# Splitting the normalised input once per layer instead of once per sweep

## The chip, the cores and the metric

The kernel runs on one core of a Trainium2 chip. The metric is the device time of one execution in microseconds (us). A core has five engines, each with its own queue of instructions, which it takes in order: TensorE (PE; PEld is its weight load), VectorE (DVE), ScalarE (ACT), GpSimd (POOL) and SyncE (SP). In this kernel all transfers between DRAM and the memory on the chip are issued by SP.

## What is computed

The reference is a trunk of two layers over 2048 tokens of width 1024. Each layer normalises its input, projects it once, and hands the columns to four groups of heads:

```python
h = rms_norm(x, ln_g)
proj = jnp.einsum('bsd,dn->bsn', h, w_in)
(a_q, a_k, a_v, a_g, b_cq, b_ckv, b_kr, b_g,
 c_q, c_k, c_v, c_g, c_iq, c_ik, c_iw, d_q, d_k, d_v, d_g) = jnp.split(proj, split_points, axis=-1)
y_a = stick_breaking(...)          # group A
y_b = softmax_attention(...)       # group B, queries and keys from normed latents
y_c = dsa_attention(...)           # group C, softmax over the 256 keys that an indexer scores highest
y_d = rms_norm(diff_attention(...), diff_subln_g) * (1.0 - lam_init)   # group D
y = jnp.concatenate([silu(a_g) * y_a, silu(b_g) * y_b, silu(c_g) * y_c, silu(d_g) * y_d], axis=-1)
return x + jnp.einsum('bsn,nd->bsd', y, w_out)
```

All of it is float32.

## The kernel before

**Products in two parts.** TensorE multiplies numbers in a rounded form of float32 (`F32R`). To keep float32 accuracy the kernel splits both factors: `hi` is the number rounded, `lo` is what the rounding leaves, and a projection (`proj`, lines 256, 257 and 260) sums hi·hi, hi·lo and lo·hi: for each of eight blocks of 128 features two matmuls with the block of `h_hi`, then eight more with `h_lo`. `split` (line 195) makes the parts: a copy that rounds, by GpSimd (`pcopy`, line 193) or ScalarE (line 200), and a subtraction, by GpSimd (`psub`, line 187) or VectorE (line 204).

**Sweeps.** The tokens are 16 tiles of 128. A layer is seven sweeps over the tiles, in the order `a h d0 d1 b c o`. Sweep a normalises and transposes the input (`a_load`), does group A and the indexer's scores, and starts the searches for the 256 highest scores. Sweep h makes the latents of group B and the gates of A and B. Sweeps d0 and d1 do two heads of group D each, and the gates of C and D. Sweep b is group B's attention, c is group C's, and o is the output projection. The last searches run in sweeps h and d0 (`SEARCH`), on ScalarE (line 538, a count of scores by their sign) and VectorE (lines 601 to 622, steps on a few numbers per token).

**Where the input goes.** `a_load` leaves the normalised, transposed tile `hf` in the buffer `x4a` (lines 331 to 334), stores it to a DRAM tile `hT` (line 335), and splits it for its own use (line 337): on GpSimd, but for the very first tile. The sweeps h, d0, d1 and c, four in each layer and so 128 times in all, load `hT` into `x4a` again (line 234) and split it again (line 236). Who splits is set by hand: ScalarE and VectorE (`"ad"`) take the even tiles in h, tiles 0 to 6 in d0, 4 to 10 in d1 and 4 to 9 in c, which is 28 tiles of a layer's 64; GpSimd (`"pp"`) takes the other 36.

**Buffers.** `x4a` is one buffer of 4 KB per partition and serves other uses too (the input tile of `a_load`, the mask of group C, the tile of sweep o). `h_hi` and `h_lo` are two buffers each, so that a third tile's parts can be written only when the first's projection has read its own. A tile's load is asked for four tiles ahead of its attention, the projection three, and the transposes to the attention's layout two (`drive`).

**Order.** `drive` interleaves the generators of loads, projections, transposes and attention by costs written into them, and a scheduler that simulates the program (`schedule_with_timeline_sim=True`) then sets the order on each engine. In a d sweep a tile's projection (`proj_d`) is followed by the root mean square of its heads (`rs`, lines 271 and 272, on GpSimd), the rotation tables (`tab`, line 190, GpSimd), the rotation on VectorE, and the split of queries and keys into `hl` (lines 997 and 998, GpSimd by lines 193 and 187). TensorE's transposes of `hl` (line 283) wait for that. GpSimd also does a fifth of the difference of the two softmaxes (lines 1070 and 1071, `rw`).

Of the kernel before, what the change touches and what calls it, by code (L numbers as in the profile page):

```python
# [10 lines left out]
F32 = mybir.dt.float32  # L11
# [49 lines left out]
def merge(*gens):  # L61
    """Interleaves generators, whose first item is their whole cost and whose others are costs of steps."""
    act = []
    for g in gens:
        if g is None:
            continue
        tot = next(g)
        act.append([0.0, max(tot, 1.0), g])
    while act:
        a = min(act, key=lambda t: t[0] / t[1])  # L70
        try:
            a[0] += next(a[2])
        except StopIteration:
            act.remove(a)
# [15 lines left out]
class Share:  # L90
    """A generator taken in shares of its cost."""
# [16 lines left out]
class Trunk:  # L108
    def __init__(self, ctx, tc, I, out, layers=2):
# [11 lines left out]
        self.hT = [dt([128, KT, 128], F32, name=f"hT{i}") for i in range(NT)]  # L121
# [40 lines left out]
    def g2(self, shape, dtype=F32):  # L162
        """scratch of the projections, up to 2 KB"""
        return self.wk.tile(shape, dtype, name="g2", bufs=4)

    def pt(self, shape, dtype=F32):
        """scratch of the attention's inner loops, up to 2 KB"""
        return self.wk.tile(shape, dtype, name="pt", bufs=3)

    def o2(self, shape, dtype=F32):  # L170
        """scratch of the attention's results, up to 2 KB"""
# [23 lines left out]
    def split(self, hi, lo, raw, eng="pp"):  # L195
        """hi: raw rounded, lo: what that leaves"""
# [9 lines left out]
    def weights(self, W, key, src, pieces, n, kt=KT, first=False):  # L206
        """src [kt*128, cols] in DRAM; pieces (column, count) side by side make n columns."""
# [3 lines left out]
        for k in range(kt):  # L211
            # the very first ones come all at once, through the memory of the rows
# [15 lines left out]
    def early(self, i, n):  # L228
        """who splits: ScalarE and VectorE while the attention of tile i leaves them time, else GpSimd"""
        return "ad" if FROM <= i < n else "pp"  # L230

    def get_h(self, i, eng="pp"):
        hf = self.x4("a", [128, KT, 128])
        self.nc.sync.dma_start(hf, self.hT[i])
        hi, lo = self.h_tiles()
        self.split(hi, lo, hf, eng)
        return hi, lo

    def load_h(self, l, i, st):
        yield 1.0  # L240
        st["h", i] = self.get_h(i, "pp" if i % 2 else "ad")

    def load_c(self, l, i, st):
        yield 1.0
        st["h", i] = self.get_h(i, self.early(i, EARLY[0]))

    def load_d(self, l, i, st):
        yield 1.0
        st["h", i] = self.get_h(i, self.early(i + 4 * (FROM > 0 and st["half"] == 0), EARLY[1]))
# [13 lines left out]
    def rstd(self, who, ss, n, width):  # L263
        """(ss / width + eps) ** -0.5 of [128, n]"""
# [10 lines left out]
    def transposes(self, dst, srcs, eng="act", tag="pj"):  # L275
        """srcs: up to four [128, m] fp32 views; dst [m, len, 128] view."""
# [3 lines left out]
        # sources of rounded results are rounded themselves  # L280
# [8 lines left out]
    def piece(self, st, key, i, shape, dtype=F32):  # L289
        """the tile of key that holds token tile i, of four each; last but one dim of shape is 4 tiles long"""  # L290
# [5 lines left out]
    def at(self, offset, g):  # L296
        """generator g, its instructions scheduled as if they came offset instructions later"""
# [17 lines left out]
    def a_load(self, l, i, st):  # L315
        """x tile -> normalised, transposed, split"""
# [18 lines left out]
        nc.sync.dma_start(self.hT[i], hf)  # L335
        hi, lo = self.h_tiles()
        self.split(hi, lo, hf, "ad" if l == i == 0 else "pp")
        st["h", i] = hi, lo
# [19 lines left out]
    def functions_a(self):  # L358
        """has ScalarE take the set of functions with both exponential and logarithm"""
        self.nc.scalar.preload_act_table_set("natural_log_exp_and_others")  # L360

    def a_first(self, l, i, st):
# [33 lines left out]
        for r in range(2):  # L396
# [6 lines left out]
            if zr is not None:  # L403
                # what is left of the stick after these blocks is at most exp(X0 - z0)
# [63 lines left out]
    def hilo64(self, u):  # L468
        """u [128, 5, 64]: [hi lo] of the first four, [hi hi] and [lo lo] of the last"""
# [9 lines left out]
    def ci_score(self, l, i, st, tied=True):  # L479
        """scores of tile i into a row buffer"""  # L480
# [3 lines left out]
        # the general search takes two more rows  # L484
# [3 lines left out]
        for c0 in range(0, n, 512):  # L488
            w = min(512, n - c0)
            # equal scores of zero rank by their index  # L490
# [25 lines left out]
    def ci_search(self, l, b):  # L516
        """per row of the tiles of b a threshold with 249..256 scores at or above it, then the 256th itself"""
# [17 lines left out]
        def count(dst, th):  # L535
            """number of scores at or above th"""
# [922 lines left out]
```

## Time and profile before

| | us |
|---|---|
| median of three runs | 4274.78 |
| lowest and highest | 4272.74, 4277.41 |
| the profiled execution, its span | 4276.6 |

The profiled execution has its span as its time: the instructions run from its first to its last microsecond. Its sweeps are told apart by the instructions that only one of them has. In the first layer, a runs to about 447 us, h to 660, d0 to 960, d1 to 1257, b to 1627, c to 1946 and o to 2145; in the second layer, a ends at 2560, h at 2787, the two d sweeps at 3085 and 3377, b at 3746, c at 4063. The projections of a sweep's first tiles lie in the sweep before.

How to read the rows: a row of a timeline is an instruction with its start and length; what stands in brackets is how long its engine stood still before it and what ended that. The chain of waits follows the program back from its last instruction, at each step to what released it. PEclk is the clock that TensorE was granted, as a share of 2.4 GHz; the other level is 1.2 GHz, so that 0.62 is a stretch that was mostly at the lower one.

### The profile page before, as it was taken

The numbers are of one execution on the slowest core, as the hardware profiler recorded it, in microseconds if no ns is written. First come the engines' busy times: TensorE is split into PE (matmuls) and PEld (weight loads), VectorE is DVE, ScalarE is ACT, GpSimd is POOL, SyncE is SP. The second block draws the span as 40 slices with busy tenths as digits, with TensorE's granted clock in tenths as the row PEclk, the third lists the DMA queues.
The fourth block names the chain that finished last, engine by engine and source line by source line (L and its number), as shares of the span: only waits on it lengthen the run. The fifth ranks groups of instructions, "written<-read, shape, count | busy, mean of one in ns | idle before, by whom it ended". The sixth has DMA issues, their size and how long they took to land.

```text
span 4276.6 us, 75274 instructions
## 1 busy us (share of the span) xinstructions
PE 3937.6 (92%) x25833; PEld 3249.9 (76%) x25833; DVE 2906.3 (68%) x10326; ACT 2371.9 (55%) x4846; POOL 1650.7 (39%) x2350
## 2 busy tenths in 40 slices
PE   6999996899988999999989999979999889999999
PEld 6877786777866777777878787867788667777777
DVE  3798788787875655663337988887968766555622
ACT  3656677465665545454126667765666655554621
POOL 2333423665664433420033343337747544344100
PEclk9999997899988999999999999979999899999999
DMA  3222531121110002114522225311211100021144
GB/s 104 80 77 84 175 112 58 50 59 52 50 35 26 19 23 68 50 44 139 167 88 81 81 91 172 114 54 48 61 53 49 36 22 18 26 74 46 59 138 139
DMA packets 204842, 312.60 MB, mean 73 GB/s; under 512 B 63777, under 2 KB 147873, under 8 KB 203937
## 3 DMA queue, kind: packets, MB, share of 16 engines
q1 hardware_dynamic: 204448, 307.69, 22.7%
q8 instruction: 206, 3.38, 0.3%
q14 instruction: 188, 1.53, 0.1%
HBM read 211.89 MB, written 95.72 MB: 72 GB/s over the span
## 4 chain that ended last, share of the span: by engine, by line
PE 57%; DVE 20%; ACT 6%; POOL 6%; DMA 5%; issue 5%; SPq 0%; DVEq 0%; ACTq 0%; POOLq 0%
PE y L866 9%; PE s L837 8%; PE tp L283 7%; PE pj L256 7%; PE pj L257 6%; PE pj L260 6%; PE s L256 3%; PE s L257 3%; PE s L260 3%; ACT junk L538 2%; DVE sc L506 2%; DVE rw L843 2%; PE pj L283 2%; DMA w_raw<-w_in 2%; DVE rw L841 2%
## 5 line engine op out<-in xcount | busy, mean ns | idle before, releaser
L256 PE MATMUL pj<-w_hi,h_hi 128*128 128x384 f32 (+4 forms) x2560 | 880.2, 352 | 51.5 <-POOL w_hi L193 22.9
L257 PE MATMUL pj<-w_lo,h_hi 128*128 128x384 f32 (+4 forms) x2560 | 863.9, 345 | 8.0 <-DVE w_lo L204 4.0
L847 ACT ACTIVATE rw<-rw,at_mn 128x896 f32<-128x896 f32 (+15 forms) x512 | 615.7, 1204 | 173.1 <-DVE at_mn L846 148.2
L285 ACT COPY pt<-tp 128x512 f32<-128x512 f32 (+3 forms) x689 | 358.1, 529 | 467.8 <-PE tp L283 390.3
L256 PEld LDWEIGHTS pj<-w_hi,h_hi 128*128 128x128 f32 x2560 | 505.7, 198 | 88.9 <-POOL w_hi L193 26.0
L283 PE MATMUL tp<-ident,rw 128*128 128x128 f32 x3264 | 540.4, 287 | 34.4 <-DVE rw L1074 20.3
L257 PEld LDWEIGHTS pj<-w_lo,h_hi 128*128 128x128 f32 x2560 | 505.3, 197 | 32.4 <-DVE w_lo L204 6.6
L260 PE MATMUL pj<-w_hi,h_lo 128*128 128x384 f32 (+4 forms) x2560 | 523.4, 338 | 0.0
L283 PEld LDWEIGHTS tp<-ident,rw 128*128 128x128 f32 x3264 | 365.4, 143 | 172.2 <-issue 117.5
L843 DVE TENSOR_SCALAR_CACHE_REDUCE rw<-s 128x512 f32<-128x512 f32 x576 | 383.0, 684 | 108.2 <-PE s L837 73.7
L260 PEld LDWEIGHTS pj<-w_hi,h_lo 128*128 128x128 f32 x2560 | 434.1, 190 | 25.7 <-issue 10.8
L271 POOL TENSOR_SCALAR rs<-ss 128x2 f32<-128x2 f32 (+4 forms) x224 | 61.7, 276 | 802.8 <-DVE ss L987 202.7
L538 ACT ACTIVATE junk<-sg,st_T 128x1152 int8<-128x1152 f32 (+4 forms) x224 | 293.9, 1312 | 83.9 <-DVE st_T L622 56.9
L272 POOL TENSOR_TENSOR rs<-rs,mhalf 128x8 f32<-128x8 f32 (+5 forms) x256 | 317.0, 1239 | 16.9
L287 DVE COPY pt<-tp 128x512 f32<-128x512 f32 (+3 forms) x247 | 152.9, 619 | 197.6 <-PE tp L283 163.5
L837 PE MATMUL s<-dk,qa 96*128 96x512 f32 (+3 forms) x640 | 233.5, 424 | 43.9 <-DVE rw L843 22.3
L187 POOL TENSOR_TENSOR h_lo<-x4a,h_hi 128x1024 fp32r<-128x1024 f32 x103 | 255.5, 2480 | 39.4 <-PE pj L260 22.8
L193 POOL TENSOR_SCALAR hl<-g 128x256 fp32r<-128x256 f32 (+1 forms) x384 | 151.2, 408 | 286.9 <-DVE g L452 61.3
L837 PE MATMUL s<-bk,qa 128*128 128x512 f32 (+6 forms) x960 | 257.8, 394 | 1.2 <-DVE at_mn L841 0.7
L283 PE MATMUL pj<-identr,hl 128*128 128x128 f32 (+1 forms) x1280 | 174.6, 258 | 74.1 <-POOL hl L187 47.9
L193 POOL TENSOR_SCALAR h_hi<-x4a 128x1024 fp32r<-128x1024 f32 x103 | 115.2, 1119 | 319.8 <-PE pj L257 156.1
L841 DVE CUSTOM_DVE_ANT_0 rw<-s,maskR 128x128 f32<-128x128 f32 (+3 forms) x400 | 187.7, 478 | 56.7 <-PE s L837 55.5
(267 smaller groups left out, 8731.5 us busy)
## 6 DMA issues: line engine op xcount, KB each, us to landing
x4a<-hT SPq DMA_DIRECT2D x128, 512.0 KB, 3.5
x4a<-x SPq DMA_DIRECT2D x32, 512.0 KB, 3.5
hT<-x4a SPq DMA_DIRECT2D x32, 512.0 KB, 2.6
x4a<-y SPq DMA_DIRECT2D x32, 512.0 KB, 3.5
x4b<-gate SPq DMA_DIRECT2D x32, 512.0 KB, 3.6
x4c<-x SPq DMA_DIRECT2D x32, 512.0 KB, 4.1
y<-o SPq DMA_DIRECT2D x96, 128.0 KB, 2.1
w_raw<-w_in SPq DMA_DIRECT2D x48, 192.0 KB, 2.6
```

The lines of the kernel that those rows point to most:

```text
L256: nc.tensor.matmul(p[:, :n], hi[:, k, :], whi[k], start=(k == 0), stop=False)
L257: nc.tensor.matmul(p[:, :n], hi[:, k, :], wlo[k], start=False, stop=False)
L260: nc.tensor.matmul(p[:, :n], lo[:, k, :], whi[k], start=False, stop=(k == kt - 1))
L272: nc.gpsimd.tensor_tensor(r, r, self.mhalf[:, :n], op=OP.pow)
L283: nc.tensor.transpose(p[:m, j, :].bitcast(dst.dtype), s.bitcast(dst.dtype), ident)
L285: nc.scalar.copy(dst, p[:m, :len(srcs), :])
L538: nc.scalar.activation(self.junk[:, :ns[g]], Sg[g], AF.Sign, bias=th[:, g:g + 1], scale=-1.0, accum_out=dst[:, g:g + 1])
L837: nc.tensor.matmul(p[:, :w], x, y, start=(k == 0), stop=(k == len(ops) - 1))
L841: nc.vector.tensor_tensor_reduce(o, p[:, :w], b, -scale, 3.0e38, OP.add, OP.min, m)
L843: nc.vector.tensor_scalar(o, p[:, :w], -scale, None, op0=OP.mult, op1=OP.min, accum_out=m)
L847: nc.scalar.activation(rw, rw, AF.Exp, bias=mn, scale=-1.0, accum_out=ls)
L866: nc.tensor.matmul(y[o:o + 64, :], v(j), pt[:, c * m:(c + 1) * m, :].rearrange("p a b -> p (a b)"), start=(j < 2), stop=(j >= nb - 2), ski ...
```

## The change

The DRAM tile `hT` becomes twice as large and holds both parts. `a_load` splits first, and then stores `h_hi` and `h_lo`, in two transfers of 512 KB where there was one. The four later sweeps load both parts straight into `h_hi` and `h_lo`, in two transfers of 512 KB where there was one, and split nothing. The choice of who splits falls away.

```diff
-        self.hT = [dt([128, KT, 128], F32, name=f"hT{i}") for i in range(NT)]
+        self.hT = [dt([128, 2, KT, 128], F32, name=f"hT{i}") for i in range(NT)]
...
-    def get_h(self, i, eng="pp"):
-        hf = self.x4("a", [128, KT, 128])
-        self.nc.sync.dma_start(hf, self.hT[i])
+    def get_h(self, i):
         hi, lo = self.h_tiles()
-        self.split(hi, lo, hf, eng)
+        for j, t in enumerate((hi, lo)):
+            self.nc.sync.dma_start(t.bitcast(F32), self.hT[i][:, j])
         return hi, lo

     def load_h(self, l, i, st):
         yield 1.0
-        st["h", i] = self.get_h(i, "pp" if i % 2 else "ad")
+        st["h", i] = self.get_h(i)
...
     def load_c(self, l, i, st):
         yield 1.0
-        st["h", i] = self.get_h(i, self.early(i, EARLY[0]))
+        st["h", i] = self.get_h(i)

     def load_d(self, l, i, st):
         yield 1.0
-        st["h", i] = self.get_h(i, self.early(i + 4 * (FROM > 0 and st["half"] == 0), EARLY[1]))
+        st["h", i] = self.get_h(i)
...
         for c in range(2):
             nc.vector.tensor_mul(hf[:, 4 * c:4 * c + 4, :], ps[c],
                                  self.gain[l][:, 4 * c:4 * c + 4, None].to_broadcast([128, 4, 128]))
-        nc.sync.dma_start(self.hT[i], hf)
         hi, lo = self.h_tiles()
         self.split(hi, lo, hf, "ad" if l == i == 0 else "pp")
+        for j, t in enumerate((hi, lo)):
+            nc.sync.dma_start(self.hT[i][:, j], t.bitcast(F32))
         st["h", i] = hi, lo
```

The rest of the diff takes out comments, so that lines after 225 stand one lower or one higher than before. The order of instructions changes in three places that matter here.

On GpSimd, in sweep d0 of the first layer, these rows stood in one run before (`rs` root mean squares, `tab` rotation tables, `hl` split queries and keys of one tile; `h_hi` and `h_lo` the split input of a later tile):

```order
L272 TENSOR_TENSOR rs<-rs,mhalf 128x8
L272 TENSOR_TENSOR rs<-rs,mhalf 128x2
L193 TENSOR_SCALAR h_hi<-x4a 128x1024
L190 TENSOR_TENSOR tab<-ci_cs,gain 128x2x32 x2
L187 TENSOR_TENSOR h_lo<-x4a,h_hi 128x1024
L193 TENSOR_SCALAR hl<-g_8751 128x4x64
L193 TENSOR_SCALAR hl<-g_8751 128x4x2x32
L187 TENSOR_TENSOR hl<-g_8751,hl 128x4x32 x2
```

and the same tile's rows stand so now:

```order
L271 TENSOR_TENSOR rs<-rs,mhalf 128x8
L271 TENSOR_TENSOR rs<-rs,mhalf 128x2
L190 TENSOR_TENSOR tab<-ci_cs,gain 128x2x32 x2
L193 TENSOR_SCALAR hl<-g_8721 128x4x64
L193 TENSOR_SCALAR hl<-g_8721 128x4x2x32
L187 TENSOR_TENSOR hl<-g_8721,hl 128x4x32 x2
```

The two rows of the input's split are gone, and nothing has taken their place between `tab` and `hl`.

On SP, in sweep a of the first layer, one tile's transfers stood so before (`sc` scores, `y` results of group A, `x4a<-x` the next input tile, `sg` scores for a search, `ci_cs` rotation tables; in brackets what SP waits for, the DMA lanes among it):

```order
L512 DMA sc_172<-sc 128x768 [waits DMAHW5_49,DVE_49]
L433 DMA y_92<-o_2152 128x256 [waits Activation_49]
L320 DMA x4a<-x 128x1024 [waits DMAHW4_49,PE_49,Pool_49]
L524 DMA sg<-sc_172 128x768 [waits DMAHW5_49,DMAHW0_49]
L446 DMA ci_cs<-c_rope 128x128 [waits DMAHW1_49,DVE_49]
L335 DMA hT_79<-x4a 128x1024 [waits DMAHW2_49,DVE_49]
```

and stand so now:

```order
L512 DMA sc_172<-sc 128x768 [waits DMAHW4_49,DVE_49]
L433 DMA y_92<-o_2160 128x256 [waits Activation_49]
L337 DMA hT_78<-h_lo 128x1024 [waits DMAHW6_49,Pool_49]
L319 DMA x4a<-x 128x1024 [waits DMAHW7_49,PE_49]
L524 DMA sg<-sc_172 128x768 [waits DMAHW4_49,DMAHW0_49]
L446 DMA ci_cs<-c_rope 128x128 [waits DMAHW1_49,DVE_49]
L337 DMA hT_79<-h_hi 128x1024 [waits DMAHW2_49,Pool_49]
L337 DMA hT_79<-h_lo 128x1024 [waits DMAHW3_49,Pool_49]
```

The store waits for GpSimd's split where it waited for VectorE's product, and the store of `h_lo` stands ahead of the next tile's load.

On SP in sweep d0 a load stood so before (`gate` the gates of a tile, `out_of` a search's result):

```order
L234 DMA x4a<-hT_77 128x1024
L1099 DMA y_87<-o_8446 128x128
L1168 DMA gate_123<-g_8645 128x256
L234 DMA x4a<-hT_78 128x1024
L1027 DMA ci_cs<-c_rope 128x2x32
```

and stands so now:

```order
L1168 DMA gate_123<-g_8617 128x256 [waits DMAHW5_49,Activation_49]
L1027 DMA ci_cs<-c_rope 128x2x32 [waits DMAHW6_49,Pool_49]
L1099 DMA y_88<-o_8595 128x128 [waits DMAHW7_49,DVE_49]
L642 DMA out_of_195<-ge 128x1664 [waits DMAHW0_49,DVE_49]
L235 DMA h_hi<-hT_78 128x1024 [waits DMAHW1_49,PE_49]
L235 DMA h_lo<-hT_78 128x1024 [waits DMAHW2_49,PE_49]
L1168 DMA gate_124<-g_8792 128x256 [waits DMAHW3_49,Activation_49]
```

Both loads wait for TensorE, which has to have read the pair of buffers that they fill, and stand ahead of the store of the gates that the same tile's projection ends with.

## Rows read from the trace of the kernel before

**Rows 1.** Page, parts 1 and 4: engines' busy time; last-ending chain by engine.

```profile
PE 3937.6 (92%) x25833; PEld 3249.9 (76%) x25833; DVE 2906.3 (68%) x10326; ACT 2371.9 (55%) x4846; POOL 1650.7 (39%) x2350
PE 57%; DVE 20%; ACT 6%; POOL 6%; DMA 5%; issue 5%; SPq 0%; DVEq 0%; ACTq 0%; POOLq 0%
```

**Rows 2.** Windows h, d0, d1, first layer: us, busy (count) per engine, PEclk, DMA.

```profile
447.00:660.00 213.00, 195.29 (x913) 164.49 (x912) 170.43 (x803) 154.60 (x303) 67.96 (x87) 0.97 0.43 141
660.00:960.00 300.00, 256.93 (x1732) 223.82 (x1732) 246.93 (x923) 183.46 (x382) 167.24 (x230) 0.86 0.18 54
960.00:1257.00 297.00, 275.80 (x2046) 231.03 (x2046) 236.24 (x798) 190.74 (x418) 176.98 (x246) 0.96 0.15 46
```

**Rows 3.** Tiles h_hi, h_lo: engine, operation, count, ns min/median/max of the splits.

```profile
L193 POOL TENSOR_SCALAR h_hi<-x4a x103: 1040/1048/1477, 51.0 to 3935.9; 128x1024 fp32r<-128x1024 f32 x103
L200 ACT CAST h_hi<-x4a x57: 1028/1047/1066, 29.9 to 3829.5; 128x1024 fp32r<-128x1024 f32 x57
L187 POOL TENSOR_TENSOR h_lo<-x4a,h_hi x103: 2347/2410/4387, 52.1 to 3939.9; 128x1024 fp32r<-128x1024 f32 x103
L204 DVE TENSOR_TENSOR h_lo<-x4a,h_hi x57: 1196/1224/1496, 31.6 to 3830.9; 128x1024 fp32r<-128x1024 f32 x57
```

**Rows 4.** Chain by line: 660 to 1257, 2787 to 3377, 1627 to 1946 us.

```profile
by line: PE pj L256 10.4%; PE pj L257 9.6%; PE pj L260 8.5%; PE y L866 7.7%; issue 6.9%; PE tp L283 6.1%; DVE rw L843 5.8%; PE s L837 5.7%; DVE rw L1074 3.1%; ACT junk L538 2.9%; POOL rs L272 2.7%; DVE rw L841 2.6%; POOL h_lo L187 2.5%; PE 
by line: PE pj L256 10.0%; PE pj L257 9.1%; PE pj L260 7.9%; PE y L866 7.2%; issue 6.4%; DVE rw L843 6.3%; PE tp L283 6.0%; PE s L837 5.1%; DVE rw L1074 3.1%; DVE rw L841 2.8%; POOL h_lo L187 2.5%; ACT rw L847 2.5%; POOL rs L272 2.2%; POOL 
by line: PE y L866 18.8%; PE tp L283 18.1%; PE s L837 14.6%; PE pj L256 5.9%; PE pj L257 5.6%; PE pj L260 5.4%; DVE rw L841 4.2%; issue 3.5%; DMA w_raw<-w_out 2.2%; PE y L878 1.9%; PE pj L283 1.8%; DVE h_lo L204 1.7%; DMA x4a<-out_of 1.4%; 
```

**Rows 5.** Timeline in d0, GpSimd, then TensorE: start us, us, what [idle before].

```profile
744.59 1.04 POOL L193 TENSOR_SCALAR h_hi<-x4a 128x1024 fp32r<-128x1024 f32 x1
...
746.32 2.38 POOL L187 TENSOR_TENSOR h_lo<-x4a,h_hi 128x1024 fp32r<-128x1024 f32 x1
748.66 2.54 POOL L193 TENSOR_SCALAR hl<-g 128x256 fp32r<-128x256 f32 x2
751.17 0.87 POOL L187 TENSOR_TENSOR hl<-g,hl 128x128 fp32r<-128x128 f32 x2
...
751.68 0.66 PE L283 MATMUL pj<-identr,hl 128*96 128x128 f32 x4 [2.90 <-POOL hl L187]
```

**Rows 6.** Window around Rows 5, columns as in Rows 2.

```profile
742.00:753.00 11.00, 4.99 (x31) 3.76 (x30) 10.96 (x18) 2.25 (x5) 10.04 (x10) 0.62 0.28 92
```

**Rows 7.** Line 602 over the whole run; two instructions of sweep h, timeline.

```profile
L602 DVE TENSOR_SCALAR st_dn<-st_T x112: 149/161/2422, 151.3 to 2846.8; 128x2 f32<-128x2 f32 x112
...
524.30 2.43 POOL L187 TENSOR_TENSOR h_lo<-x4a,h_hi 128x1024 fp32r<-128x1024 f32 x1
524.33 2.42 DVE L602 TENSOR_SCALAR st_dn<-st_T 128x2 f32<-128x2 f32 x1
```

**Rows 8.** Pieces of the chain in order of time: start us, us, what.

```profile
467.94 2.31 DVE st_L L577
...
568.97 2.43 DVE st_T L622
```

**Rows 9.** TensorE's waits, 660 to 1257 us: total us, times, longest.

```profile
PE pj L283 <- POOL hl L187: 18.8, 14, 5.4
```

**Rows 10.** Timeline of TensorE in sweep h: one pair's last use, its next first use.

```profile
555.34 2.03 PE L260 MATMUL pj<-w_hi,h_lo 128*128 128x512 f32 x8
...
568.88 0.44 PE L256 MATMUL pj<-w_hi,h_hi 128*128 128x416 f32 x1
```

**Rows 11.** DMA queue: packets, MB, share; transfers of tile hT to landing.

```profile
q1 hardware_dynamic: 204448, 307.69, 22.7%
...
DMA to landing us min/median/max: 2.6/3.4/8.5
```

**Rows 12.** SyncE's waits over the whole run: total us, times, longest.

```profile
SPq L335 <- DVE x4a L333: 144.9, 21, 13.9
SPq L320 <- DMA hT<-x4a: 36.8, 15, 3.7
```

## The prediction

> **What bounds the kernel now.** I read the page first, then the windows by sweep, then the chain of waits in the sweeps that the change touches, then the timeline at its largest pieces. On the page TensorE's matmuls are busy 92% of the span, VectorE 68%, and the chain that ended last lies 57% on PE, 20% on DVE, 6% each on ACT and POOL and 5% on DMA [rows 1]. That is an average. By sweeps, b and o hardly touch what is changed, and the d sweeps are where PE is held up: of d0's 300 us its matmuls are busy 257, of d1's 297 they are busy 276, so 64 us of standstill in the first layer's two, and the granted clock is 0.86 and 0.96 there [rows 2]. In sweep h, PE stands still for 18 us of 213 [rows 2].
>
> What holds PE up in the d sweeps is seen in one place. From 744.6 us GpSimd runs the rounding copy of a later tile's input, 1.04 us, and its subtraction, 2.38 us, ahead of the split of the present tile's queries and keys, for which PE's transposes wait; PE stands still 2.90 us before them [rows 5]. In the 11 us around it GpSimd is busy 10.0, VectorE 10.96, PE 5.0, and the granted clock is 0.62, so mostly 1.2 GHz [rows 6]. So the input's split does lie on the path there, though no page total shows it.
>
> **The change, part by part.**
>
> *What goes.* 128 splits. GpSimd did 103 in all, of which 31 are group A's own and stay: 72 x (1.048 + 2.410) = 249 us off GpSimd. ScalarE did 57 copies and VectorE 57 subtractions, of which one each stays: 56 x 1.047 = 59 us and 56 x 1.224 = 69 us [rows 3]. Most of it ran beside PE's work, so these 377 us are no forecast; what counts is the part on the chain.
>
> *Piece 1, GpSimd in the d sweeps.* GpSimd's subtraction of the split is 2.5% of the chain in the first layer's d sweeps (597 us) and 2.5% in the second's (590 us) [rows 4]: 14.9 + 14.8 = 29.7 us.
>
> *Piece 2, VectorE stopped by GpSimd.* In sweep h, a search step on two numbers per token, 0.161 us at the median, took 2.42 us: it began 0.03 us after GpSimd's subtraction of 2.43 us and ended with it [rows 7]. The chain of the first layer's sweep h holds four such pieces of 2.31 to 2.43 us, the first and the last of which are shown [rows 8]: 4 x (2.35 - 0.16) = 8.8 us. The second layer's h runs on PE by its chain, so I count none there.
>
> The Trainium skill (SBUF — State Buffer, "Who interferes with whom") states that a VectorE instruction in a two-port mode, or one with two SBUF inputs, and a GpSimd instruction block each other for the whole of whichever came first, and that transfers block no engine. The trace agrees on the first: 2.42 us beside 2.43 [rows 7]; on the second no run here says anything. By that rule every VectorE instruction of these kinds that meets a split gets shorter, not the four alone, which speaks for the first rival below.
>
> *Piece 3, sweep c.* VectorE's subtraction of the split is 1.7% of the chain over the first layer's 319 us of sweep c [rows 4]: 5.4 us, and I take the same for the second layer: 11 us.
>
> *What of this comes back.* 29.7 + 8.8 + 11 = 49.5 us on the chain. When a piece goes, what was second latest sets the time. The one place that shows how much is gained is the standstill above: PE stood 2.90 us where the split had taken 3.42 us of GpSimd [rows 5], which is 0.85. It is one of the larger standstills, so I round down to 0.8: 40 us. From below, TensorE's transposes in the first layer's d sweeps waited for `hl` 18.8 us in 14 waits [rows 9], and only some of those have a split ahead of them; if a quarter does, both layers give 9 us.
>
> *What is added: transfers.* 128 loads and 32 stores of 512 KB more, 84 MB beside the 307.7 MB that take 22.7% of the 16 engines' span [rows 11]; at the same price, 6 points more. Each load of 512 KB lands in 3.4 us at the median, 8.5 at most [rows 11]. I take 7 us for the two parts together, and 8.5 as the bad case. What hides this is the second pair of buffers. In sweep h, where a tile is shortest, the last use of one pair ends at 555.34 + 2.03 = 557.4 us and the same pair is needed at 568.9 [rows 10]: 11.5 us, in which the load fits. (The rounded part is free earlier, and the rest is needed later than that.) In the d sweeps tiles are longer: 16 in 300 us, 19 us each [rows 2]. Cost: nothing. Were that cover gone, the loads would cost up to 3.5 us a tile, 128 times. Below nothing I see no effect of the loads.
>
> *What is added: waits.* SP now stands at each load until PE has read the pair. Behind it stand the store of the gates, which the same projection ends with, rotation tables for the next tile and results. They become due at about that moment or are wanted a tile later; I take nothing, and up to 0.3 us a tile, 40 us, for the far end, from the waits that SP has at such places now (36.8 us in 15 waits at one, some 2.5 us each [rows 12]). The store in sweep a now waits for GpSimd's split; that is a rival below. The next tile's load into `x4a` no longer waits for the store to land, 36.8 us of SP's time [rows 12], which lies off the path as far as rows show; I take nothing.
>
> *What moves.* The order on PE changes in sweeps a, d0, d1 and c, and not in b and o. The same d sweeps take 597 us in one layer and 590 in the other, with the same work in another order [rows 4]; so I give the order 10 us either way, and no sign.
>
> **Sum.** 4276.6 - 40 = 4236.6 for the profiled execution. Its span is 1.8 us above the median of the runs, so I forecast 4235 us by the median, 0.9% less; between 4215 and 4266 I call it this case.
>
> **The rivals.**
>
> *The relief is larger, by the clock.* The windows of d0 and d1 have 0.86 and 0.96 of the clock [rows 2]: 300 x 0.14 + 297 x 0.04 = 54 us a layer that PE has lost, 108 in both. If all 49.5 us come back, with GpSimd's copy beside its subtraction (1.05 of 2.41 x 29.7 = 13 us), and a quarter of the clock's loss, 27 us: 4275 - 90 = 4185 us. For it: in the window around the standstill VectorE and GpSimd are both full [rows 6], and the clock is low in that very place. Against it: most of the 64 us has other causes, the softmax's rows on DVE first (line 843 is 5.8% of that chain [rows 4]).
>
> *It is hidden.* What PE waited for arrives no earlier, since VectorE's rotation, not GpSimd, sets when `hl` can start. Then the lower bound holds, 9 us or less: 4266 to 4275. For it: PE's waits for `hl` are 18.8 of 64 us [rows 9]. Against it: in the case shown GpSimd had no pause from the copy to `hl` [rows 5].
>
> *Slower: the stores of sweep a hold SP.* SP stands at the old store 144.9 us, waiting for VectorE's product [rows 12]. The new stores wait 1.05 and 2.41 us longer, for the split [rows 3], and behind the second stands the next tile's input load. 32 tiles x 3.46 = 111 us if all of it lies on the path. Against it: that load waited for the same split before, since it fills the buffer that the split reads. It decides from the point at which SP comes to a tile's tables or input later than that tile's first matmuls want them; with half the tiles, 55 us lost and 40 gained: 4290 us.
>
> **How the numbers follow.** The forecast 0.45, larger relief 0.25, hidden 0.16, slower by the stores or by a worse order in the same sweeps 0.14. The range reaches from the first rival's 4185 to the edge of the slower case: 4184 to 4282; below lies 0.07, above 0.13. A measurement here tells about 0.2%, 8.5 us: faster means under 4266, slower over 4283. The first two cases are faster, and a little of the hidden one: 0.71; the hidden case's rest 0.15; slower 0.14.
>
> **What would show it.** Right: 72 fewer splits on GpSimd; TensorE's waits for `hl` in the first layer's d sweeps under 12 us; no search step in sweep h at 2.4 us, unless beside a weight's split; d windows of 597 and 590 us some 12 to 18 us shorter each, h 4 to 8 us shorter in the first layer, c some 4 each, b and o within 2; granted clock of d0 above 0.86; TensorE waiting under 10 us in all for loaded parts. Wrong: sweep a longer by over 10 us in a layer, with SP at the stores and PE or ACT waiting for the input load or tables; PE waiting for a load in h; or d windows unchanged with the waits for `hl` gone and VectorE's rows in their place.

## The result

The kernel after takes 4235.6 us by the median of four runs (4221.5 to 4242.2); the kernel before took 4275.4 beside it. The ratio is 0.9897, 95% interval 0.9877 to 0.9917: faster by 1.0%. The forecast was 4235.

The rows of the page of after that answer to [rows 1, 3, 11]: the span, the busy time of each engine with its share and instructions, the DMA queue (packets, MB, share of 16 engines), and issues with KB each and us to landing.

```profile
span 4230.8 us, 75339 instructions
...
PE 3925.9 (93%) x25833; PEld 3246.6 (77%) x25833; DVE 2789.1 (66%) x10270; ACT 2318.9 (55%) x4790; POOL 1363.8 (32%) x2206
...
q1 hardware_dynamic: 227488, 391.59, 29.3%
...
h_hi<-hT SPq DMA_DIRECT2D x128, 512.0 KB, 3.8
h_lo<-hT SPq DMA_DIRECT2D x128, 512.0 KB, 4.9
```

PE is busy 12 us less, at the same count. GpSimd has 144 instructions and 287 us less, ScalarE 56 and 53, VectorE 56 and 117. The queue moves 84 MB more and is busy 6.6 points more.

The windows of after, columns as in [rows 2] (us, busy time and instructions of PE, PEld, DVE, ACT, POOL, the granted clock, DMA share, GB/s): the first layer's h, both its d sweeps together, the second layer's, the first layer's c, and last the first 300 us of the first layer's d sweeps, to set beside d0.

```profile
435.00:651.00 216.00, 200.00 (x939) 170.12 (x937) 148.51 (x754) 143.09 (x295) 45.00 (x75) 0.96 0.57 178
651.00:1238.00 587.00, 529.64 (x3775) 455.15 (x3775) 461.68 (x1769) 370.03 (x795) 265.85 (x436) 0.92 0.27 80
2758.00:3338.00 580.00, 528.14 (x3803) 453.77 (x3803) 458.50 (x1668) 353.25 (x779) 270.14 (x452) 0.92 0.27 82
...
1606.00:1922.00 316.00, 305.08 (x2191) 231.75 (x2191) 186.60 (x605) 170.69 (x316) 83.13 (x132) 0.99 0.26 81
...
651.00:951.00 300.00, 260.99 (x1780) 227.56 (x1780) 243.03 (x1008) 192.89 (x396) 125.49 (x212) 0.89 0.29 86
```

The d sweeps take 587 and 580 us where they took 597 and 590 (from the sweep's first matmul, as in the table below, 587 and 579 where they took 595 and 590). The clock changed little: 0.89 in the first 300 us, where d0 had 0.86 [rows 2], and 0.92 over both sweeps, where it was 0.91; in the second layer's it was 0.93 and is 0.92. By these windows the first layer's h is not shorter: 216 us, where it took 213 [rows 2]. What is shorter is the sweep a ahead of it, 435 us where it took 447.

TensorE's waits for `hl`, total us, times, longest. First the kernel before in the second layer's d sweeps, 2787 to 3377 us (the first layer's 18.8 is [rows 9]):

```profile
PE pj L283 <- POOL hl L187: 20.5, 14, 5.6
```

then after in the first layer's d sweeps, 651 to 1238 us, and in the second's, 2758 to 3338 us:

```profile
PE pj L282 <- POOL hl L187: 7.6, 5, 3.1
...
PE pj L282 <- POOL hl L187: 13.7, 9, 3.2
```

39.3 us have become 21.3. What is left has no split of the input in it. GpSimd's timeline in d0 of after ahead of the longest of these waits in the first layer (start us, us, instruction, in brackets idle time before it and what ended that), and TensorE's transposes that wait:

```profile
743.55 0.20 POOL L270 TENSOR_SCALAR rs<-ss 128x8 f32<-128x8 f32 x1 [9.00 <-DVE ss L987]
743.84 1.64 POOL L271 TENSOR_TENSOR rs<-rs,mhalf 128x8 f32<-128x8 f32 x1
745.44 0.78 POOL L190 TENSOR_TENSOR tab<-ci_cs,gain 128x64 f32<-128x64 f32 x2
...
747.01 0.78 POOL L193 TENSOR_SCALAR hl<-g 128x256 fp32r<-128x256 f32 x2
747.75 0.70 POOL L271 TENSOR_TENSOR rs<-rs,mhalf 128x2 f32<-128x2 f32 x1
748.42 0.87 POOL L187 TENSOR_TENSOR hl<-g,hl 128x128 fp32r<-128x128 f32 x2
...
748.93 1.09 PE L282 MATMUL pj<-identr,hl 128*96 128x128 f32 x8 [3.07 <-POOL hl L187]
```

GpSimd was idle for 9 us and waited for VectorE's sum of squares (`ss`). In [rows 5] it had no pause: the input's split stood in front. But [rows 5] is not how most of the waits before came about. By GpSimd's timeline, its split stood ahead of `hl`, without a pause of GpSimd over 0.3 us in between, in 10 of the 28 waits of both layers' d sweeps, 12.9 of the 39.3 us. The longest of [rows 9], 5.4 us, came so (VectorE, GpSimd, TensorE of the kernel before):

```profile
723.79 1.22 DVE L204 TENSOR_TENSOR h_lo<-x4a,h_hi 128x1024 fp32r<-128x1024 f32 x1
...
725.54 0.42 DVE L1043 TENSOR_TENSOR g<-g,x4c 128x256 f32<-128x256 f32 x1
...
728.02 0.41 DVE L991 TENSOR_TENSOR g<-g,rs 128x256 f32<-128x256 f32 x1
...
728.60 0.78 POOL L193 TENSOR_SCALAR hl<-g 128x256 fp32r<-128x256 f32 x2 [3.13 <-DVE chkC L641]
...
729.85 0.66 PE L283 MATMUL pj<-identr,hl 128*96 128x128 f32 x4 [5.42 <-POOL hl L187]
```

GpSimd stood idle for 3.13 us, and what it waited for was the rotation (lines 1043 and 991) on VectorE, with VectorE's own subtraction of a later tile's input, and search and softmax work, in between.

The search steps. Line 602 over the whole run of after (the answer to [rows 7]), and two instructions of its sweep a that still meet:

```profile
L602 DVE TENSOR_SCALAR st_dn<-st_T x112: 149/161/296, 150.9 to 2798.2; 128x2 f32<-128x2 f32 x112
...
157.86 2.41 POOL L187 TENSOR_TENSOR h_lo<-x4a,h_hi 128x1024 fp32r<-128x1024 f32 x1
157.89 2.41 DVE L603 TENSOR_SCALAR st_nd<-st_T 128x2 f32<-128x2 f32 x1
```

Which step meets a split is the order's doing, so the count says more than one line. Of the steps on two numbers per token, 24 took over 1.5 us before, 16 in the sweeps a and 8 in h; after, 11 do, all in sweep a, where GpSimd's own split for that sweep remains. In the runs below, 21 to 24 do in each kernel with all splits and 9 to 13 in each with none; with GpSimd's alone taken away 11, with the others' alone 21.

Last, SyncE's waits over the whole run of after (total us, times, longest), to [rows 12]:

```profile
SPq L235 <- PE pj L256: 611.0, 96, 18.0
SPq L337 <- POOL h_hi L193: 245.9, 31, 17.3
```

These are the largest rows of each line; all rows together, SP stands at the loads (line 235) for 834 us and at the stores (line 337) for 296. Among TensorE's waits of the whole run, no row names a loaded part, so that standing doesn't reach it through the loads. Something behind SP does come later: VectorE's waits for a search's results (`out_of`, line 630) grow from 7.8 to 23.4 us. No run shows whether that costs time.

### The profile page after: what moved, and what is told of

Same layout as the page of the kernel before. It is cut to its first block, busy times and chain, and to the rows that moved or that the text cites. A ratio compares the mean times of both kernels' runs of the same rounds, so it can differ in the third digit from the quotient of the medians.

```text
span 4230.8 us, 75339 instructions
## 1 busy us (share of the span) xinstructions
PE 3925.9 (93%) x25833; PEld 3246.6 (77%) x25833; DVE 2789.1 (66%) x10270; ACT 2318.9 (55%) x4790; POOL 1363.8 (32%) x2206
## 5 line engine op out<-in xcount | busy, mean ns | idle before, releaser
L259 PE MATMUL pj<-w_hi,h_lo 128*128 128x384 f32 (+4 forms) x2560 | 535.9, 339 | 0.0
L270 POOL TENSOR_SCALAR rs<-ss 128x2 f32<-128x2 f32 (+4 forms) x224 | 49.9, 223 | 1074.7 <-DVE ss L911 250.5
L187 POOL TENSOR_TENSOR hl<-g,hl 128x128 fp32r<-128x128 f32 (+1 forms) x384 | 215.7, 577 | 0.3
L866 PE MATMUL y<-pt,dv 128*64 128x128 f32 x2176 | 194.4, 305 | 19.8 <-DVE o L1097 12.4
```

Of the source, the lines that this page charges most:

```text
L187: self.nc.gpsimd.tensor_sub(o, a, b)
L259: nc.tensor.matmul(p[:, :n], lo[:, k, :], whi[k], start=False, stop=(k == kt - 1))
L866: nc.tensor.matmul(y[o:o + 64, :], v(j), pt[:, c * m:(c + 1) * m, :].rearrange("p a b -> p (a b)"), start=(j < 2), stop=(j >= nb - 2), ski ...
```

## The experiments

**One table for all.** Lengths of the sweeps in the profiled execution of each kernel, first and second layer, us. The sweeps are parted by TensorE's first instruction of a kind (keys of D, of B, of C, the output projection's first, and for the second layer's start group A's first product after the exponentials). The medians are of the runs, the ratios are to the kernel before in the same comparison (its medians 4275 to 4278).

| kernel | median us | ratio, 95% interval | a+h | d | b | c |
|---|---|---|---|---|---|---|
| before | 4275.4 | | 662, 583 | 595, 590 | 370, 370 | 320, 316 |
| before_ord | 4270.7 | 0.9986 [0.9974, 0.9998] | 648, 584 | 596, 591 | 369, 366 | 319, 315 |
| before_xst | 4305.7 | 1.0069 [1.0043, 1.0096] | 668, 590 | 601, 593 | 370, 370 | 319, 315 |
| part_pool | 4255.6 | 0.9953 [0.9936, 0.9969] | 651, 582 | 591, 575 | 370, 364 | 319, 316 |
| part_ad | 4272.6 | 0.9990 [0.9980, 1.0000] | 656, 583 | 589, 595 | 370, 367 | 316, 318 |
| after | 4235.6 | 0.9897 [0.9877, 0.9917] | 651, 578 | 587, 579 | 368, 362 | 316, 316 |
| after_ord | 4221.7 | 0.9865 [0.9839, 0.9892] | 650, 579 | 581, 573 | 370, 363 | 318, 317 |
| raw_store | 4214.4 | 0.9860 [0.9843, 0.9876] | 647, 574 | 579, 571 | 370, 362 | 314, 319 |
| one_dma | 4227.4 | 0.9887 [0.9871, 0.9904] | 646, 577 | 579, 576 | 370, 364 | 317, 317 |
| dead_touch | 4241.0 | 0.9933 [0.9908, 0.9958] | 649, 583 | 588, 572 | 369, 362 | 321, 315 |
| dead_pool | 4277.5 | 1.0004 [0.9995, 1.0014] | 649, 586 | 608, 595 | 370, 361 | 317, 316 |
| dead_ad | 4274.7 | 0.9995 [0.9983, 1.0007] | 653, 585 | 599, 575 | 370, 370 | 323, 325 |
| dead_all | 4383.0 | 1.0247 [1.0230, 1.0264] | 655, 599 | 637, 619 | 371, 368 | 331, 331 |
| one_p30 | 4213.7 | 0.9849 [0.9824, 0.9875] | 645, 574 | 581, 581 | 366, 365 | 313, 316 |

The theory under test: the time went with the engine time of the splits, GpSimd's first of all. The rivals: a luckier order of the same work; and, on the other side, that waits for transfers cost something.

### Half of the splits taken out of the kernel before

Sweep a of the kernel before also stores both parts; one kind of tile loads them, the other still loads the raw tile and splits it.

```diff
+        for j, t in enumerate((hi, lo)):
+            nc.sync.dma_start(self.parts[i][:, j], t.bitcast(F32))
...
     def get_h(self, i, eng="pp"):
+        if eng == "pp":        # part_pool; "ad" in part_ad
+            hi, lo = self.h_tiles()
+            for j, t in enumerate((hi, lo)):
+                self.nc.sync.dma_start(t.bitcast(F32), self.parts[i][:, j])
+            return hi, lo
```

part_pool, expected:

> The kernel before, in which sweep a also stores both parts, and the 72 tiles that GpSimd split later load the parts; the 56 of ScalarE and VectorE still load the raw tile and split it. Theory of the prediction (GpSimd's and VectorE's subtraction on the path; GpSimd's share of the sum is 29.7 + 8.8 of 49.5): 4275 less 20 to 40, 4235 to 4255. Rival, that order alone moved the time: anywhere from 4235 to 4295, with no tie to which engine is freed. Rival, that nothing but both halves together helps: 4270 to 4280.

part_ad, expected:

> The mirror of the run part_pool: the 56 tiles that ScalarE and VectorE split load the parts, GpSimd still splits its 72 from the raw tile. Theory of the prediction: VectorE's share is 11 of 49.5, so 4262 to 4272. By the runs that put work back (each half cost 40): 4230 to 4245. Rival, order alone: anywhere from 4235 to 4295.

Measured: 4255.6, 22 us less than the 4278.0 beside it, and 4272.6, 5 us less. Both lie half a microsecond above the theory's upper ends, 4255 and 4272, and part_ad far above the 4230 to 4245 that the runs with work put back had promised. Set beside the kernel before, GpSimd's half carries most of it, as forecast, and both together give 40 in the kernel after, 12 more than the sum of the two. By themselves the two medians don't exclude the rival of the order, and part_ad can't be told from no change; two other views and runs do more.

There is a closer comparison. part_pool, part_ad and two kernels of a later section, before_xst and raw_store, all store the raw tile and both parts in sweep a. They differ only in who loads parts instead of splitting: nobody in before_xst (4305.7), everybody in raw_store (4214.4). From the one to the other GpSimd's 72 splits are worth 50 us when they go first (to 4255.6) and 58 when they go second (from 4272.6); the other engines' 56 are worth 33 and 41. By this square the second half is not small. Each of the four is one order, so that each step carries its luck.

TensorE's waits for `hl` in the d sweeps, first and second layer, in part_pool:

```profile
PE pj L289 <- POOL hl L188: 17.0, 14, 3.7
...
PE pj L289 <- POOL hl L188: 19.2, 16, 4.8
```

and in part_ad:

```profile
PE pj L289 <- POOL hl L188: 15.2, 10, 8.3
...
PE pj L289 <- POOL hl L188: 10.4, 12, 4.2
```

36.2 and 25.6 us, where before has 39.3, before_ord 35.5 and before_xst 42.1. With GpSimd's splits gone, `hl` comes about as late as ever; it comes earlier where the others' are gone. So in the kernel before most of these waits hung on the splits by ScalarE and VectorE, not on GpSimd's. Yet it is part_pool whose d sweeps are shorter than before's in both layers (table).

part_pool shows one thing that no order explains. In it VectorE executes the same 10326 instructions as before [rows 1]; its page:

```profile
PE 3922.5 (92%) x25833; PEld 3237.4 (76%) x25833; DVE 2843.8 (67%) x10326; ACT 2372.8 (56%) x4846; POOL 1382.1 (33%) x2206
```

VectorE is busy 2843.8 us, not 2906.3, 62.5 us less; before_ord and before_xst, other orders with all splits, have 2904.5 and 2908.8. Put back (dead_pool below), the 72 make 81.9 us more of after's 2789.1, again with the same number of instructions. The largest group in the 62.5 is the scaling of queries and keys by `rs` in the d sweeps, the first row from before, the second from part_pool (busy us and mean ns of 64):

```profile
L991 DVE TENSOR_TENSOR g<-g,rs 128x256 f32<-128x256 f32 x64 | 40.1, 627 | 27.0 <-POOL rs L272 26.7
```

```profile
L999 DVE TENSOR_TENSOR g<-g,rs 128x256 f32<-128x256 f32 x64 | 29.6, 463 | 14.7 <-POOL rs L278 14.4
```

The Trainium skill (SBUF — State Buffer, "Who interferes with whom") says that such a VectorE instruction, with two SBUF inputs, and one of GpSimd that reads SBUF exclude each other for the whole of whichever came first. The run agrees: 164 ns less on each of the 64 by the mean, and the longest, 2.40 us before, is 0.61; in part_ad, where GpSimd still splits, it is 2.52. The same rows show what GpSimd's split does in its own queue: VectorE's waits for `rs` ahead of this scaling fall from 26.7 to 14.4 us. They are 21 to 27 in the four kernels in which GpSimd splits its 72 tiles from the raw input, and 14 to 19 in part_pool and the five that do no split.

### Splits put back into the kernel after as useless work

Each load is followed by a copy and a subtraction whose result nobody reads, on the engines of the old table: all (dead_all), GpSimd's 72 tiles (dead_pool), the 56 of ScalarE and VectorE (dead_ad). dead_touch has all of them, on one column each.

```diff
     def get_h(self, i, eng="pp"):
...
+        self.dead(hi.bitcast(F32), lo.bitcast(F32), eng)
...
+    def dead(self, a, b, eng):
+        d = self.x4("a", [128, KT, 128], F32R)
+        if eng == "pp":
+            self.pcopy(d, a)              # dead_touch: d[:, 0, :1], a[:, 0, :1]
+            self.psub(d, b, a)
+        else:
+            self.nc.scalar.copy(d, a)
+            self.nc.vector.tensor_sub(d, b, a)
```

dead_all, expected:

> The changed kernel with the 128 splits put back as dead work: each of the four later sweeps still loads both parts, and then the engines that split before (GpSimd for 72 tiles, ScalarE and VectorE for 56) copy and subtract the loaded parts into the buffer x4a, which nobody reads. If the 40 us came from the engines' time (the theory), the time goes back to 4265 to 4285 us. If they came from the order of the work, from x4a being free or from the loads (the rival), it stays at 4228 to 4244 us.

dead_pool, expected:

> The changed kernel with dead splits for GpSimd's 72 tiles alone (copy and subtraction into x4a); the 56 tiles of ScalarE and VectorE have none. The theory puts GpSimd's pieces (its subtraction ahead of the queries' and keys' split, and VectorE stopped by it) at 0.8 x 38.5 = 31 us: 4258 to 4272 us. If VectorE's own subtractions were what mattered, 4234 to 4245 us. The rival (order, not engine time): 4228 to 4244 us.

dead_ad, expected:

> The changed kernel with dead splits for the 56 tiles of ScalarE (copy) and VectorE (subtraction) alone. The theory puts these at 0.8 x 11 = 9 us: 4240 to 4250 us. If VectorE's time is what mattered instead of GpSimd's, 4256 to 4270 us. The rival (order, not engine time): 4228 to 4244 us.

dead_touch, expected:

> The kernel after with the same 512 useless instructions as in the run dead_all (copy and subtraction for each of the 128 loads, same engines, same buffer, same waits), but of one column each, so that they keep the buffer and the queues' order without engine time. If engine time made dead_all slow (4383): 4215 to 4260. If it was the wait for the loaded parts and for the buffer at the head of the queues: 4330 to 4390. Order alone puts it anywhere within 20 of 4235.

(The useless instructions are 256, not 512: two for each of the 128 loads.) Measured: 4383.0, 4277.5, 4274.7 and 4241.0. The first three are all above what was expected, so the sizes were misjudged; dead_ad lies even above the 4256 to 4270 of "VectorE's time is what mattered". GpSimd's work put back costs 42 us, the other engines' 39, both together 147. The same instructions with the same waits but without the work cost 5. So engine time in these places costs that much. It doesn't follow that the same splits cost as much where the kernel before had them: taken out there, the other engines' half gave 5 us by part_ad, or 33 and 41 by the square above.

Two views tell more. The copies of dead_touch on GpSimd (busy us, mean ns, then idle time before them and what ended it):

```profile
L193 POOL TENSOR_SCALAR x4a<-h_hi 128x1 fp32r<-128x1 f32 x72 | 19.9, 276 | 276.4 <-DMA h_hi<-hT 255.6 <-DVE st_rc L620 6.3 <-DVE st_sp L632 5.2
```

GpSimd's queue stands 255.6 us for the loads, and it costs next to nothing. TensorE's waits for `hl` over the whole run, in before, after, dead_touch and dead_all, in this order:

```profile
PE pj L283 <- POOL hl L187: 47.9, 39, 5.6
```

```profile
PE pj L282 <- POOL hl L187: 23.9, 19, 3.2
```

```profile
PE pj L293 <- POOL hl L187: 31.4, 31, 6.0
```

```profile
PE pj L293 <- POOL hl L187: 60.0, 39, 10.0
```

With all the work back, `hl` is late again. By halves, dead_pool has 34.3 us in all and dead_ad 23.7, no more than after: what dead_ad costs goes another way, which no run shows. That dead_all is 107 us slower than the kernel before, which did the same splits, isn't settled: its splits begin only when a load has landed and hold the queue through the work, but no run divides the two further than dead_touch does.

### Order alone, and stores alone

One constant of the planner (how much later transposes count) goes from 10 to 12, in both kernels; no work changes.

```diff
-LATER = {"search": -30, "prep": 10, ...}
+LATER = {"search": -30, "prep": 12, ...}
```

before_ord, expected:

> The kernel before with one constant of the planner moved (the transposes' instructions count as 12 later in place of 10), which changes the order of about a third of TensorE's instructions and no work. It shows how far an order without a reason moves the time: within 10 of 4276 by the prediction's term for the order, within 25 by the run raw_store.

after_ord, expected:

> The same constant moved in the kernel after: within 10 of 4236 by the prediction's term for the order, within 25 by the run raw_store. If the gain of the change were a lucky order, this run would fall back towards 4276.

before_xst is the kernel before with the two stores of the parts (the first piece of the diff of part_pool), which nobody loads. raw_store is its counterpart: the kernel after with the old store of the raw tile put back, to a DRAM tile that nobody loads.

before_xst, expected:

> The kernel before with the two stores of the parts in sweep a as well (nobody loads them): the counterpart of the run raw_store on the kernel before. It has the stores of the change without its loads and with all splits. If the stores, or what they do to the order, bring part of the gain: 4250 to 4268. If they cost: 4282 to 4295. If neither: 4270 to 4282.

raw_store, expected:

> The changed kernel with the old store put back beside the two new ones: in sweep a the unsplit tile is stored too, from x4a, to DRAM that nobody reads, so that x4a is held until that store has landed, as before. If the first layer's sweep a became shorter because x4a came free earlier, the time rises by 6 to 13 us, 4242 to 4249 us. If sweep a gained by the order or by the later sweeps' splits being gone, nothing: 4228 to 4240 us.

Measured: before_ord 4270.7 (6 less), after_ord 4221.7 (14 less), before_xst 4305.7 (29 more), raw_store 4214.4 (21 less than after). Two of the four are misses. raw_store, with more work, is faster than either range, and before_xst is dearer than any of its three. after_ord is beyond the 10 of the prediction. The luck of an order is larger than I had it, but it doesn't explain the gain: the three kernels that do all splits on their tiles lie at 4271 to 4306, the five that do none (after, after_ord, raw_store, one_dma, dead_touch) at 4214 to 4241. The worst of the one group is 30 us below the best of the other, and by the means of the groups the change is worth 56. Pairs that differ by the change alone give 40 (before and after), 49 (with the constant moved in both) and 91 (before_xst and raw_store, which store the same). TensorE's waits for `hl` in both layers' d sweeps part the groups too: 35 to 42 us with all splits, 14 to 24 with none.

Do the stores cost the 29 us? SP's waits at the stores of the parts, over the whole run: first before_xst, then raw_store.

```profile
SPq L340 <- POOL h_lo L188: 45.3, 21, 3.6
...
SPq L340 <- POOL h_hi L194: 27.4, 29, 1.4
```

```profile
SPq L339 <- POOL h_lo L188: 46.4, 22, 3.4
...
SPq L339 <- POOL h_hi L194: 27.8, 29, 2.0
```

SP stands there equally long, 73 and 74 us, in a kernel that is 29 us slower than its neighbour and in one that is 21 us faster. And by the table 9 us of the loss lie in the d sweeps, which store no parts; 13 lie in a and h. So the stores' waits do not set it; that it is the order is what remains, argued and not shown.

### One transfer instead of two

```diff
-        return (self.wk.tile([128, KT, 128], F32R, name="h_hi"), self.wk.tile([128, KT, 128], F32R, name="h_lo"))
+        t = self.wk.tile([128, 2, KT, 128], F32R, name="h_hl")
...
-        for j, t in enumerate((hi, lo)):
-            self.nc.sync.dma_start(t.bitcast(F32), self.hT[i][:, j])
+        self.nc.sync.dma_start(t.bitcast(F32), self.hT[i])
```

> The kernel after with both parts in one tile, so that a load is one transfer of 1 MB and a store is one of 1 MB, where there were two of 512 KB each. If SP's issue of 128 more loads and 32 more stores or the later landing of the second part cost something: 4222 to 4232. If not: 4236, moved by order by up to 20 either way. If the later release of the parts (the buffer of h_hi is free before that of h_lo) matters: 4240 to 4260.

Measured: 4227.4, 8 less than after. That is in the range for a cost of SP's issue or of the second landing, and as well inside the spread of orders, so it can't tell the two apart. The load lands in 5.1 us, and the later release of the buffer costs nothing that can be seen:

```profile
h_hl<-hT SPq DMA_DIRECT2D x128, 1024.0 KB, 5.1
```

### GpSimd's freed time used

```diff
-POOLED = 0.2
+POOLED = 0.3
```

> The kernel of the run one_dma with three tenths of the difference of the two softmaxes on GpSimd, where it is two tenths, since the splits have left GpSimd 15 to 20 points of its time in the d sweeps and VectorE stays busy there nearly all the time. If VectorE's own work is what bounds the d sweeps now: 4200 to 4220, d 4 to 8 shorter each. If GpSimd's blocking of VectorE eats it, or GpSimd comes late with its part: 4228 to 4250.

(By the windows GpSimd's busy share of the d sweeps fell by 12 points, not 15 to 20, and VectorE is busy 79% of them in after.) Measured: 4213.7, 14 us less than one_dma, but not for the reason given: the d sweeps are 2 and 5 us longer (table). VectorE's part of the difference at full width, in one_dma and then in one_p30:

```profile
L1073 DVE SCALAR_TENSOR_TENSOR rw<-rw,d_c 128x512 f32<-128x512 f32 x192 | 165.1, 896 | 2.1
```

```profile
L1073 DVE SCALAR_TENSOR_TENSOR rw<-rw,d_c 128x512 f32<-128x512 f32 x152 | 143.5, 974 | 1.9
```

An instruction of the same width takes 974 ns instead of 896, and over all widths VectorE has 16 instructions fewer and no less time: 211.5 us where it had 208.0. So the theory falls there; what it gained elsewhere is of the size of an order's luck. one_p30 and raw_store are the two fastest, both faster than before and after, and neither can be said to be better than the other by its design.

## Why the prediction was right, and where not

**The sum.** 40 us were forecast for the change and the medians differ by 39.8. The profiled execution lost 45.8 us (4276.6 to 4230.8; forecast 4236.6). The closeness is luck: by other orders of the same work the gain would have come out at 30 (4271 to 4241) to 91 us (4306 to 4214), by the means of the groups at 56. And the pieces differ from what the sum put in them. By the table the pair's gain is 19 us in d (forecast 24), 16 in a and h (7), 10 in b (nothing) and 4 in c (9), less 3 in o.

**Piece 1, the d sweeps: about the right size, by another way than the one read.** Forecast 24 us for both layers (29.7 x 0.8). The pair gives 8 + 11, below the 12 to 18 each that I had named as the sign. Over the three orders with all splits and the five without, the table's means are 597 and 591 against 583 and 574: 14 and 17 us, 31 together. It is the one gain that each order shows in both layers. TensorE's waits for `hl` fell, as said: from 39.3 to 21.3 us, and the 7.6 in the first layer is below the 12 named. The step that failed is the path: the one place of [rows 5], GpSimd's split in front of `hl`, was taken for the whole piece. The split stood there in a third of these waits (12.9 of 39.3 us), and part_pool without it still has 36.2. What GpSimd's splits cost in d, by part_pool, was elsewhere: VectorE's scaling waited 12 us longer for `rs` and took 10 us longer beside them. How that reaches TensorE is not shown. And the splits by ScalarE and VectorE, on which most of the waits for `hl` hung, stand in the sum at nothing for the d sweeps.

**Piece 2, sweep h: right in kind, the size not shown.** 7 us were forecast for the first layer and none for the second. Parted where TensorE ends its last product of group A (line 424 of the kernel before), h went from 189 to 185 and from 185 to 182 us, and a from 473 to 466 and from 398 to 396; by the windows above, h did not get shorter in the first layer at all. The kernel before_ord, with all splits, has 186 for the first layer's h and 462 for its a, as short as the kernels without splits. So the 11 us that the pair gained in the first layer's a and h can be order. By the means of the groups a and h together are 11 and 8 us shorter. What is clear of the order is the mechanism: the eight stretched search steps of h, five in the first layer and three in the second, are gone, and so they are in every kernel in which GpSimd doesn't split. That the second layer has three of them and some of the gain speaks against counting none there.

**Piece 3, sweep c: wrong.** 9 us were forecast; by the means c is 317 with all splits and 317 without. A 1.7% share of the chain was taken for time that comes back at four fifths; none came. dead_ad, where such splits make c 7 and 9 us longer than in after, shows that they can lie on the path there; where the kernel before had put them, they did not. The profiled pair's own 4 us in the first layer are within the orders' spread.

**Not forecast: sweep b.** I had said that b stays within 2 us. The second layer's is shorter by 8 in the pair and by 6 in the means (369 to 363), the first layer's is not. No run explains it, since sweep b has no use of the loads, and only c's first tiles are loaded near its end. It is no wait: TensorE stands still 24 us in it before and 25 in after_ord. It stays open.

**What was taken at nothing.** The loads: right. No wait of TensorE names one, the parts land in 3.8 and 4.9 us, each from its own issue, where I took 7 for both, and the queue's share rose by 6.6 points where 6 were worked out. SP's standing: 834 us at the loads without a wait of TensorE for them; VectorE's 16 us more of waits for search results are the one thing behind it that grew much, at a price that is not shown.

**The order: mis-sized.** 10 us either way, taken from two layers' d sweeps, was too little: 4271 to 4306 with the splits, 4214 to 4241 without.

**The rivals.** Larger relief by the clock, 4185: no. The clock of d0 rose from 0.86 to 0.89 and that of the first layer's d sweeps from 0.91 to 0.92, that of the second's did not rise; the sign that I had named is there, the 27 us are not. Hidden: not by its price, 9 us or less, for the two groups are 30 us apart at their nearest. But its mechanism, that VectorE's rotation and not GpSimd sets when `hl` can start, is what part_pool and the wait of 5.4 us show, and its guess that a quarter of the waits have a split ahead was close to the third measured. What it left out is VectorE's own time: in the first layer's d sweeps its busy time went from 483 to 462 us. Slower by the stores: no. SP stands longer at them, 296 us where it stood 205 at the old store, and sweep a is shorter and not longer. Yet before_xst shows that the side of the loss was near, for an edit that frees nothing cost 29 us.

## What to carry to other kernels

Engine time off the critical path can still be worth taking away, where it stands in a queue ahead of something on the path or stops another engine: look at what stands in front of the late instruction in its own queue, and at short instructions that take as long as a neighbour's long one. One place of a timeline shows that a mechanism exists, not how often it acts: go through all the waits of its kind, and take the halves of a change apart, as part_pool and part_ad do, before calling it the cause. A share of the chain of waits is no measure of what comes back: in the d sweeps about all of it came, in c nothing. Where a scheduler sets the order, compare groups of orders: a single pair of programs carries tens of us of luck.

## What the runs showed of the hardware

GpSimd's 72 splits of 3.5 us kept VectorE busy 62.5 us longer (taken out, part_pool) or 81.9 us longer (put back, dead_pool) with the same number of instructions, of which the chain had shown me 8.8. And one load of 1 MB landed in 5.1 us by the median, where one of 512 KB took 3.5 in the kernel before (the 3.4 of [rows 11] counts the stores too):

```profile
x4a<-hT SPq DMA_DIRECT2D x128, 512.0 KB, 3.5
```

In these two kernels the second half MB costs 1.6 us, not another 3.5, so that my 7 us for both parts was too dear.
